# Head norms by a ScalarE square root, attention's loads on GpSimd's queue and plain stick-breaking gates in a decoder block

## The chip, the cores and the metric

One core of a Trainium2 chip runs the whole program. The metric is the device time of one execution in microseconds; the time of a kernel is the median of its runs. TensorE is PE (its weight loads PEld), VectorE is DVE, ScalarE is ACT, GpSimd is POOL, and SyncE, which only issues DMAs here, is SP.

## The reference

One decoder block with D = 1024 on 1024 positions in float32. Three branches work on the normed input in parallel, are gated and summed, and an MLP follows.

```python
proj = einsum('bsd,de->bse', rmsnorm(x, g_mix_norm), w_in)
sb_q, sb_k, sb_v, fx_q, fx_k, fx_v, f_logit, m_q, gate_logit = split_columns(proj, SPLITS)
o_sb = stick_breaking_attention(heads(sb_q), heads(sb_k), heads(sb_v))        # 8 heads of 64
fq, fk = rmsnorm(heads(fx_q), g_fox_q), rmsnorm(heads(fx_k), g_fox_k)
o_fox = forgetting_attention(fq, fk, heads(fx_v), log_sigmoid(f_logit + b_forget))  # 8 of 64
mk, mv = split(einsum('bmd,de->bme', rmsnorm(mem, g_mem_norm), w_mem_kv))     # 256 tokens
o_mem = memory_attention(rmsnorm(heads(m_q), g_mem_q), rmsnorm(mk, g_mem_k), mv)  # 4 of 128
gates = sigmoid(gate_logit)                                                   # 3 x 1024
merged = gates[0] * (o_sb @ w_branch_sb) + gates[1] * (o_fox @ w_branch_fox) + gates[2] * (o_mem @ w_branch_mem)
x = x + merged @ w_out
u = relu(rmsnorm(x, g_mlp_norm) @ w_ff_up);  x = x + (u * u) @ w_ff_down
```

The root of the change is the one in `rmsnorm` of the heads of fx_q, fx_k, m_q and mk.

## The kernel before

**Products.** Each float32 operand is split in a high and a low part (`split`, L1046 and L1047: a copy on ACT, a subtraction on DVE), and a product is three passes on PE: high by high, high by low, low by high. A weight block of 128 x 1024 is fetched raw (`fetch`, L1054), then split into `whi` and `wlo`.

**Stages** in the profiled execution: the norm of x and its transposes with the first values (0 to 50 us), the keys and values of the memory (to 120), six projections `sbk, sbq, mq, fxk, fxq, sbv` (to 385) by seven products each instead of eight (`KINDS`, matmuls at L1412; their weight blocks come by `unit_loads`, L1335), attention (to 905), two branch products (to 1000), the third branch (`last_branch`, to 1100), the output product, the MLP up (L1840, to 1450) and down (L2510, to the end). Head pairs 0 to 3 are stick-breaking, 4 to 7 forgetting; the products of the gates (`dense_gate`, L1133) and the memory's attention run between them and fill PE.

**Order.** All stages up to the branches are written as coroutines in a planner. A coroutine asks for an engine with an estimated cost (`Op`), for a buffer out of a pool (`Get`), for an event, or for time to pass (`Sleep`); the planner simulates these and so writes the order of the instructions of each engine. That order is fixed at build time. On the chip an engine takes its instructions in this order, and an instruction whose semaphores are late holds all behind it. `spawn(gen, late)` gives a coroutine a priority, a lower number being earlier. `transfer` (L298) issues a DMA on SP and tells the planner when it should have landed. An `Op` for a table function of ACT adds 1.3 us to the plan when the table has to change.

**The heads' norm** (`normed_turned`, L711) takes a 128 x 512 tile of sums of squares `st` (reduced at L707) and `rsqrt_ops` makes the inverse root: an integer seed on DVE (L351, L352), then three Newton steps of four operations on POOL (L358 to L361). DVE scales the tile (L716), PE turns it by four transposes (L723), ACT and DVE split it (L729, L730). The norm of x uses `root` and `rsqrt_quick` instead: a square root on ACT (L369) and a reciprocal with one correcting step on DVE (L374 to L383).

**Loads of attention.** The turned keys and queries go through DRAM (`sbk_scr` and others). `load_pairs` (L996) fetches them for each pair and half in pieces of 64 x 512, 128 KB, into places of the pool HT; `load_v` (L1032) fetches the pair's values once all of them are stored (L1207). The output of a unit is evicted to a buffer `ob` (L956, pool OB with 2 buffers) and stored by SP (L959). Gates are evicted to `o` (L1533, `gate_put`), as a sigmoid for gates 0 to 7 and 16 to 23, plain for 8 to 15, and stored to `gate_scr` (L1537); the branches load them back. All of these issue on SP.

Of the kernel before, what the change touches and what calls it, by code (L numbers as in the profile page):

```python
# [16 lines left out]
I32 = mybir.dt.int32  # L17
# [26 lines left out]
def tile_hybrid_block(  # L44
# [253 lines left out]
    def transfer(fn, size, issue=0.1, rate=250e3):  # L298

        yield Op("SP", issue, fn, 0.0)  # L300
        machine.pipe = max(machine.now, machine.pipe) + size / rate
        yield Sleep(machine.pipe + 2.0 - machine.now)
# [42 lines left out]

    def rsqrt_ops(ss, n):

        v, y0, a_, y1 = stat(n), stat(n, I32), stat(n), stat(n)

        def seed():  # L350
            nc.vector.tensor_scalar(v, ss, EPS, None, ALU.add)  # L351
            nc.vector.tensor_scalar(y0, v.bitcast(I32), -0.5, 1597463007.0, ALU.mult, ALU.add)  # L352
        yield Op("DVE", 2 * SMALL, seed)

        def steps():
            a, b = y0.bitcast(F32), y1
            for _ in range(3):
                nc.gpsimd.tensor_tensor(a_, a, a, ALU.mult)  # L358
                nc.gpsimd.tensor_tensor(a_, a_, v, ALU.mult)  # L359
                nc.gpsimd.tensor_scalar(a_, a_, -0.5, 1.5, ALU.mult, ALU.add)  # L360
                nc.gpsimd.tensor_tensor(b, a_, a, ALU.mult)  # L361
                a, b = b, a
        yield Op("POOL", 12 * 0.2, steps)
        return y1
# [214 lines left out]
    def memory():  # L579
        yield pairs[4].made[1]  # L580

        def fetched_q(h, half):
            q = yield Get(HT, 2)

            def issue():
                for t, scr in zip(q, p_scr["mq"]):
                    nc.sync.dma_start(f32(t), scr[h * P:(h + 1) * P, half * 512:(half + 1) * 512])
            yield from transfer(issue, 2 * P * 512 * 4, 0.2)
            q_of[h, half] = q
        q_of = {}  # L590
        for c in range(2):
# [3 lines left out]
            def issue():  # L595
                for i, t in enumerate(kv):
                    nc.sync.dma_start(f32(t), m_scr[c][:, i, :])
            loaded = spawn(transfer(issue, 4 * P * 512 * 4, 0.4), -20.0)
# [112 lines left out]
    def normed_turned(raw, ss, hd, gain, fn):  # L711

        n = 512 // hd
        r = yield from rsqrt_ops(ss, n)
        raw3 = raw.rearrange("p (n d) -> p n d", d=hd)
        yield Op("DVE", dve_time(512), lambda: nc.vector.tensor_tensor(  # L716
            raw3, raw3, r.unsqueeze(2).to_broadcast([P, n, hd]), ALU.mult))
        tr = yield Get(TR)
# [122 lines left out]
    def fox_tile(pair, b, i, e):  # L841
# [8 lines left out]
        def chunk(ci, c, cols, u):  # L850
# [14 lines left out]
            yield Op("ACT", act_time(u) + 0.17, lambda: nc.scalar.activation(  # L865
# [110 lines left out]
    def load_pairs():  # L976
        yield ready
        for c, pair in enumerate(pairs):
# [5 lines left out]
            for b in range(2):  # L984
# [4 lines left out]
                def halves(half):  # L989
# [5 lines left out]
                    def put(k, rows_, src):  # L995
                        nc.sync.dma_start(f32(t[k][rows_, :]), src)  # L996
# [19 lines left out]
                evs = [spawn(transfer(k0_, 4 * HD * 2048, 0.3), -20.0), spawn(transfer(k1_, 4 * HD * 2048, 0.3), -20.0),  # L1016
# [1554 lines left out]
```

## Time and profile before

| | before |
|---|---|
| median of 3 runs | 1763.73 us (1763.01 to 1766.23) |
| profiled execution | 1765.67 us |
| its span, mean granted clock | 1763.9 us, 0.992 |
| PE busy | 1708.9 us |
| ACT busy | 895.2 us |
| POOL busy | 172.9 us |
| ACT table loads L1533, x10 | 12.8 us |

The span is the time from the first to the last instruction of one profiled execution. Busy times of engines overlap, so they do not add to the span. A wait in a view is the idle time of an engine just before an instruction, with the instruction or DMA whose semaphore came last. The granted clock is that of PE in a stretch, 1.00 being full speed.

### The profile page before, as it was taken

How to read it: one execution, taken by the hardware profiler on the slowest of the kernel's cores; microseconds unless marked ns; L12 is line 12 of the kernel's file. 1: busy time of each engine (PE TensorE's matmuls, PEld its weight loads, DVE VectorE, ACT ScalarE, POOL GpSimd, SP SyncE). 2: the span in 40 equal slices, each digit the busy share in tenths (PEclk: the TensorE clock that was granted, in tenths of full speed). 3: DMA queues.
4: the chain of work that ended last, by engine and by line, in shares of the span. 5: the costliest groups of instructions: out<-in, count | busy, mean ns of one | idle time of the engine just before them, and what ended most of it. 6: DMA issues, size and time to landing. Idle time of an engine off the chain costs nothing.

```text
span 1763.9 us, 25496 instructions
## 1 busy us (share of the span) xinstructions
PE 1708.9 (97%) x9186; PEld 1450.5 (82%) x9186; DVE 1338.7 (76%) x2243; ACT 895.2 (51%) x1612; POOL 172.9 (10%) x445
## 2 busy tenths in 40 slices
PE   9989988897999999999999999999999999999999
PEld 8978988896888888788888887878888887888887
DVE  7875677756998976688875789897777777687875
ACT  6443354444676699888862235733333344333331
POOL 0010165500000000000000001112111220000000
PEclk9999999998999999999999999999999999999999
DMA  6544432556545433653556743134444467365531
GB/s 234 176 141 156 145 105 90 164 177 199 141 120 146 142 98 109 180 164 99 160 153 208 239 169 115 53 120 159 158 144 148 144 235 261 132 209 182 199 119 72
DMA packets 175694, 271.72 MB, mean 154 GB/s; under 512 B 14992, under 2 KB 88720, under 8 KB 175568
## 3 DMA queue, kind: packets, MB, share of 16 engines
q1 hardware_dynamic: 165712, 237.33, 42.1%
q0 software_dynamic: 9856, 32.78, 5.3%
q8 instruction: 72, 1.18, 0.3%
q14 instruction: 54, 0.44, 0.1%
HBM read 181.44 MB, written 88.60 MB: 153 GB/s over the span
## 4 chain that ended last, share of the span: by engine, by line
PE 53%; issue 15%; POOL 8%; DVE 6%; DMA 3%; ACT 3%; SPq 1%; POOLq 0%; ACTq 0%; DVEq 0%
PE pp L1133 17%; PE pp L2510 7%; PE tr L2510 3%; PE sc L2510 3%; POOL s_scr L1857 3%; PE tr L921 3%; PE pv L2510 2%; PE pv L938 2%; PE sc L938 2%; POOL st L358 1%; PE pp L1840 1%; POOL st L359 1%; POOL st L360 1%; POOL st L361 1%; DVE h L1776 1%
## 5 line engine op out<-in xcount | busy, mean ns | idle before, releaser
L1133 PE MATMUL pp<-hi,whi 128*128 128x512 f32 x368 | 148.8, 404 | 0.0
L1133 PE MATMUL pp<-lo,whi 128*128 128x512 f32 x368 | 145.9, 396 | 0.0
L1133 PE MATMUL pp<-hi,wlo 128*128 128x512 f32 x368 | 145.5, 395 | 0.0
L1047 DVE TENSOR_TENSOR wlo<-raw,whi 128x1024 fp32r<-128x1024 f32 (+1 forms) x82 | 100.1, 1221 | 45.6 <-ACT whi L1046 45.5
L1046 ACT ACTIVATE whi<-raw 128x1024 fp32r<-128x1024 f32 (+1 forms) x82 | 86.4, 1056 | 87.8 <-DMA raw<-w_b 35.1
L2510 PE MATMUL pp<-h,sop 128*128 128x512 f32 x540 | 128.7, 395 | 1.1 <-DVE sop L1776 1.1
L2510 PEld LDWEIGHTS pp<-h,sop 128*128 128x128 f32 x540 | 101.1, 187 | 26.2 <-DVE sop L1776 1.6
L1840 PE MATMUL pp<-h,oh 128*128 128x512 f32 x384 | 120.9, 396 | 0.7 <-ACT cu L1926 0.6
L928 DVE TENSOR_TENSOR ptl<-tr,pth 128x512 fp32r<-128x512 f32 (+1 forms) x160 | 98.6, 627 | 21.3 <-ACT pth L926 20.1
L926 ACT ACTIVATE pth<-tr 128x512 fp32r<-128x512 f32 (+1 forms) x160 | 86.3, 559 | 19.8 <-PE tr L921 7.9
L831 DVE TENSOR_TENSOR_SCAN r<-r,sm 128x896 f32<-128x896 f32 (+5 forms) x64 | 85.6, 1346 | 7.9 <-ACT r L816 7.9
L1840 PEld LDWEIGHTS pp<-h,oh 128*128 128x128 f32 x384 | 71.8, 187 | 19.2 <-ACT cu L1926 1.5
L2428 ACT ACTIVATE h<-t 128x2048 fp32r<-128x2048 f32 x16 | 30.7, 1919 | 110.2 <-DVE t L1776 97.4
L2111 POOL TENSOR_TENSOR h<-h,gb 128x512 f32<-128x512 f32 x8 | 12.0, 1502 | 750.9 <-DMA x_scr<-h 750.9
L1133 PEld LDWEIGHTS pp<-hi,wlo 128*128 128x128 f32 x368 | 69.6, 189 | 16.7
L1133 PEld LDWEIGHTS pp<-hi,whi 128*128 128x128 f32 x368 | 70.1, 190 | 10.0
L1133 PEld LDWEIGHTS pp<-lo,whi 128*128 128x128 f32 x368 | 70.1, 190 | 10.0
L1840 PE MATMUL pp<-h,ol 128*128 128x512 f32 x192 | 76.0, 396 | 0.0
L1833 ACT ACTIVATE oh<-raw 128x512 fp32r<-128x512 f32 x64 | 39.4, 625 | 61.8 <-DVE raw L1776 61.8
L2510 PE MATMUL sc<-h,sop 128*128 128x512 f32 x264 | 63.4, 395 | 0.0
L2510 PE MATMUL tr<-h,sop 128*128 128x512 f32 x264 | 63.4, 395 | 0.0
L1133 PE MATMUL pp<-h,whi 128*128 128x512 f32 x192 | 63.0, 396 | 0.0
(615 smaller groups left out, 5071.7 us busy)
## 6 DMA issues: line engine op xcount, KB each, us to landing
ur<-s_scr SPq DMA_DIRECT2D x26, 1024.0 KB
raw<-w_in SPq DMA_DIRECT2D x50, 512.0 KB
raw<-w_up SPq DMA_DIRECT2D x60, 256.0 KB
s_scr<-s POOLq DMA_DIRECT2D x60, 256.0 KB, 2.5
g<-w_down SPq DMA_DIRECT2D x14, 1024.0 KB
s_scr<-cu POOLq DMA_DIRECT2D x48, 256.0 KB, 2.9
gate_scr<-o SPq DMA_DIRECT2D x46, 256.0 KB
o<-gate_scr SPq DMA_DIRECT2D x32, 256.0 KB
```

The costliest lines, as they stand in the source:

```text
L831: nc.vector.tensor_tensor_scan(out=rev, data0=rev, data1=zero.to_broadcast([P, n]), initial=1.0, op0=ALU.mult, op1=ALU.add)
L921: nc.tensor.transpose(tr[:, jj * 256 + a * P:jj * 256 + (a + 1) * P], es[a][:, j * P:(j + 1) * P], ident)
L926: yield Op("ACT", act_time(512 - lo_c), lambda: nc.scalar.activation(ph[:, lo_c:], tr[:, lo_c:], AF.Copy))
L928: yield Op("DVE", dve_time(512 - lo_c), lambda: nc.vector.tensor_tensor(pl[:, lo_c:], tr[:, lo_c:], f32(ph[:, lo_c:]), ALU.subtract))
L938: nc.tensor.matmul(pv[0][:, c_:256], pair.v[:, j, b, :], p_[:, jj * 256 + c_:(jj + 1) * 256], start=(k == 0 and n_ == 0 and i == 0), stop= ...
L1046: yield Op("ACT", 0.03 + act_time(m), lambda: nc.scalar.activation(hi, raw, AF.Copy))
L1047: yield Op("DVE", dve_time(m), lambda: nc.vector.tensor_tensor(lo, raw, f32(hi), ALU.subtract))
L1133: nc.tensor.matmul(ps, a_, b_, start=(first and i == 0), stop=(last and i == n - 1))
L1833: nc.scalar.activation(h_, src, AF.Copy)
L1840: nc.tensor.matmul(ps, w[a_][:, k * P:(k + 1) * P], h[b_][k], start=(first and k == 0 and i == 0), stop=(last and k == 3 and i == 2), skip ...
L1857: nc.gpsimd.dma_start(s_scr[r0:r0 + P, :], t)
L2510: nc.tensor.matmul(ps, a_[:, c, qs], b_[:, c, :], start=(kind in ("P1", "P2", "P7") and c == 0 and i == 0), stop=(kind in ("P2", "P4", "P3 ...
```

## The change

1. `rsqrt_ops` goes; `normed_turned` calls `root` on ACT and `rsqrt_quick` on DVE. The planner waits 0.8 us before it asks for the buffer of the transposes.
2. The DMAs of attention's keys, queries and values, the memory's, the projections' weight blocks, and the raw weight blocks once the memory's keys and values are made are issued by POOL. The planner's costs of an issue change with it.
3. Gates 0 to 7 are stored plain as well; the branch of stick-breaking (b == 0) takes the sigmoid after it has loaded the gate.
4. `ob` has three buffers in place of two; the memory's attention waits for the end of pair 3 in place of the keys of pair 4; `forget` starts two projections earlier; `unit_prep` has priority -4; the second load of the root table becomes a square root that reads `raw1[0]`; the planner's estimate of an exponential goes from 0.17 to 0.21.

```diff
-    def transfer(fn, size, issue=0.1, rate=250e3):
-        yield Op("SP", issue, fn, 0.0)
+    def transfer(fn, size, issue=0.1, rate=250e3, queue_="SP"):
+        yield Op(queue_, issue, fn, 0.0)
         machine.pipe = max(machine.now, machine.pipe) + size / rate
...
         return ((a[0], b[0]), (a[0], b[1]), (a[1], b[0]))
-    def rsqrt_ops(ss, n):
-        v, y0, a_, y1 = stat(n), stat(n, I32), stat(n), stat(n)
-        def seed():
-            nc.vector.tensor_scalar(v, ss, EPS, None, ALU.add)
-            nc.vector.tensor_scalar(y0, v.bitcast(I32), -0.5, 1597463007.0, ALU.mult, ALU.add)
-        yield Op("DVE", 2 * SMALL, seed)
-        def steps():
-            a, b = y0.bitcast(F32), y1
-            for _ in range(3):
-                nc.gpsimd.tensor_tensor(a_, a, a, ALU.mult)
-                nc.gpsimd.tensor_tensor(a_, a_, v, ALU.mult)
-                nc.gpsimd.tensor_scalar(a_, a_, -0.5, 1.5, ALU.mult, ALU.add)
-                nc.gpsimd.tensor_tensor(b, a_, a, ALU.mult)
-                a, b = b, a
-        yield Op("POOL", 12 * 0.2, steps)
-        return y1
...
     def memory():
-        yield pairs[4].made[1]
+        yield pairs[3].over
...
                 for t, scr in zip(q, p_scr["mq"]):
-                    nc.sync.dma_start(f32(t), scr[h * P:(h + 1) * P, half * 512:(half + 1) * 512])
-            yield from transfer(issue, 2 * P * 512 * 4, 0.2)
+                    nc.gpsimd.dma_start(f32(t), scr[h * P:(h + 1) * P, half * 512:(half + 1) * 512])
+            yield from transfer(issue, 2 * P * 512 * 4, 1.1, queue_="POOL")
             q_of[h, half] = q
...
                 for i, t in enumerate(kv):
-                    nc.sync.dma_start(f32(t), m_scr[c][:, i, :])
-            loaded = spawn(transfer(issue, 4 * P * 512 * 4, 0.4), -20.0)
+                    nc.gpsimd.dma_start(f32(t), m_scr[c][:, i, :])
+            loaded = spawn(transfer(issue, 4 * P * 512 * 4, 2.2, queue_="POOL"), -20.0)
             evs = []
...
         n = 512 // hd
-        r = yield from rsqrt_ops(ss, n)
+        z = stat(n)
+        yield Op("ACT", 0.25, lambda: root(z, ss), table=AF.Sqrt)
+        r = yield from rsqrt_quick(ss, z, n)
         raw3 = raw.rearrange("p (n d) -> p n d", d=hd)
...
             raw3, raw3, r.unsqueeze(2).to_broadcast([P, n, hd]), ALU.mult))
+        yield Sleep(0.8)
         tr = yield Get(TR)
...
             yield Op("DVE", (0.22 if c + u == n else 0.0) + dve_time(u) + SMALL, maxima)
-            yield Op("ACT", act_time(u) + 0.17, lambda: nc.scalar.activation(
+            yield Op("ACT", act_time(u) + 0.21, lambda: nc.scalar.activation(
                 e[:, c:c + u], sc[:, :u], AF.Exp, bias=nx[:, ci:ci + 1], accum_out=l[:, ci:ci + 1]), table=AF.Exp)
...
                     def put(k, rows_, src):
-                        nc.sync.dma_start(f32(t[k][rows_, :]), src)
+                        nc.gpsimd.dma_start(f32(t[k][rows_, :]), src)
                     lower, upper, f4 = slice(0, HD), slice(HD, P), slice(HD, HD + 4)
...
                 (k1_, q1_), (k0_, q0_) = halves(1), halves(0)
-                evs = [spawn(transfer(k0_, 4 * HD * 2048, 0.3), -20.0), spawn(transfer(k1_, 4 * HD * 2048, 0.3), -20.0),
-                       spawn(transfer(q1_, (3 if fox else 2) * HD * 2048, 0.3), -20.0),
-                       spawn(transfer(q0_, (3 if fox else 2) * HD * 2048, 0.3), -20.0)]
+                evs = [spawn(transfer(k0_, 4 * HD * 2048, 1.6, queue_="POOL"), -20.0), spawn(transfer(k1_, 4 * HD * 2048, 1.6, queue_="POOL"), -20.0),
+                       spawn(transfer(q1_, (3 if fox else 2) * HD * 2048, 1.2, queue_="POOL"), -20.0),
+                       spawn(transfer(q0_, (3 if fox else 2) * HD * 2048, 1.2, queue_="POOL"), -20.0)]
                 if b == 0:
...
         h0 = 2 * (pair.p % 2)
-        yield from transfer(lambda: nc.sync.dma_start(f32(pair.v), src[:, :, h0:h0 + 2, :]), P * 8192)
+        yield from transfer(lambda: nc.gpsimd.dma_start(f32(pair.v), src[:, :, h0:h0 + 2, :]), P * 8192, 0.8, queue_="POOL")
         machine.fire(pair.v_made)
...
-    def fetch(raw, load):
+    def fetch(raw, load, queue_=nc.sync):
         pieces, kk, n = load
...
             m = src.shape[1]
-            nc.sync.dma_start(view[:, :, off:off + m], src.rearrange("(k p) n -> p k n", p=P))
+            queue_.dma_start(view[:, :, off:off + m], src.rearrange("(k p) n -> p k n", p=P))
...
             raw = yield Get(RAW)
-            yield from transfer(lambda: fetch(raw, load), P * kk * n * 4)
+            if kv_over.fired:
+                yield spawn(transfer(lambda: fetch(raw, load, nc.gpsimd), P * kk * n * 4, 0.8, queue_="POOL"), -30.0)
+            else:
+                yield from transfer(lambda: fetch(raw, load), P * kk * n * 4)
         else:
...
-        yield prepped["fxk", "P1"]
+        yield prepped["sbq", "P1"]
         for ev in logits_made:
...
                 def fetched_block(u=u, key=key, raw=raw, src=src):
-                    yield from transfer(lambda: nc.sync.dma_start(
-                        raw.rearrange("p (k n) -> p k n", k=4), src.rearrange("(k p) n -> p k n", p=P)), P * 4096)
+                    yield from transfer(lambda: nc.gpsimd.dma_start(
+                        raw.rearrange("p (k n) -> p k n", k=4), src.rearrange("(k p) n -> p k n", p=P)), P * 4096, 0.8,
+                        queue_="POOL")
                     machine.fire(block_in[u, key])
...
         E.close()
-        opened("A2", (PH, "pth", 2, 512, F32R), (PL, "ptl", 2, 512, F32R), (OB, "ob", 2, 256, F32),
+        opened("A2", (PH, "pth", 2, 512, F32R), (PL, "ptl", 2, 512, F32R), (OB, "ob", 3, 256, F32),
                (ES, "es", 4, 512, F32), (OO, "o", 3, 512, F32), (HT, "h", 7, 512, F32R))
+        yield Sleep(4.0)
         pair = yield Get(WP)
...
             gt = yield Get(place)
-            func = AF.Copy if KD <= n < 2 * KD else AF.Sigmoid
+            func = AF.Copy if n < 2 * KD else AF.Sigmoid
             yield Op("ACT", act_time(512), lambda: nc.scalar.activation(gt, ps, func),
...
                     gts[d, half], gate_scr[b * D + d * P:b * D + (d + 1) * P, half * 512:half * 512 + 512]), P * 512 * 4)
+                if b == 0:
+                    yield Op("ACT", act_time(512), lambda: nc.scalar.activation(gts[d, half], gts[d, half], AF.Sigmoid),
+                             table=AF.Sigmoid)
...
         spawn(unit_loads())
-        spawn(unit_prep())
+        spawn(unit_prep(), -4.0)
         spawn(forget(), 5.0)
...
     early = []
-    root_table()
+    nc.scalar.activation(C.t("st", [P, 8])[:, :1], raw1[0][:, :1], AF.Sqrt, bias=one, scale=0.0)
...
```

How the order of instructions moves, at three places.

DVE, in the projections, at one head norm of the forgetting keys. `sn` is the tile, `st` its sums and roots, `wlo` the low part of a weight block. Before:

```order
L707 TENSOR_REDUCE st_1163<-sn_146 128x4
L351 TENSOR_SCALAR st_1181<-st_1163 128x4
L352 TENSOR_SCALAR st_1182<-st_1181 128x4
L1047 TENSOR_TENSOR wlo_164<-raw_166,whi_163 128x1024
L716 TENSOR_TENSOR sn_145<-sn_145,st_1184 128x512
```

After the change:

```order
L687 TENSOR_REDUCE st_1163<-sn_146 128x4
L354 TENSOR_SCALAR st_1202<-st_1163 128x4
L357 RECIPROCAL st_1181<-st_1181 128x4
L361 TENSOR_TENSOR st_1203<-st_1181 128x4
L362 TENSOR_TENSOR st_1203<-st_1203,st_1202 128x4
L363 SCALAR_TENSOR_TENSOR st_1204<-st_1203,st_1181 128x4
L1030 TENSOR_TENSOR wlo_164<-raw_166,whi_163 128x1024
L698 TENSOR_TENSOR sn_145<-sn_145,st_1204 128x512
```

The two operations before POOL's twelve have become five that end the root on DVE itself, and the split of a weight block still stands ahead of the scaling.

SP, at the start of attention. `h` are the places of the pair's keys and queries, `v_sb` the stored values in DRAM, `raw` a weight block. Before:

```order
L996 DMA h_4094<-sbq_scr_86 64x512
L996 DMA h_4091<-sbq_scr_85 64x512
L996 DMA h_4091<-sbq_scr_86 64x512
L1207 DMA v_sb_96<-sn_138 128x512
L1207 DMA v_sb_96<-sn_145 128x512
L1207 DMA v_sb_95<-sn_140 128x512
L1207 DMA v_sb_95<-sn_139 128x512
L1207 DMA v_sb_95<-sn_143 128x512
L1207 DMA v_sb_95<-sn_144 128x512
L1032 DMA v_4103<-v_sb_95 128x8x256
```

After the change the loads stand on the queue of POOL:

```order
L1037 DMA raw_166<-w_in 128x8x128
L979 DMA h_3873<-sbk_scr_87 64x512 x2
L979 DMA h_3872<-sbk_scr_88 64x512 x2
L979 DMA h_3876<-sbk_scr_87 64x512 x2
L979 DMA h_3875<-sbk_scr_88 64x512 x2
L979 DMA h_3874<-sbq_scr_85 64x512
L979 DMA h_3874<-sbq_scr_86 64x512
L979 DMA h_3871<-sbq_scr_85 64x512
L979 DMA h_3871<-sbq_scr_86 64x512
L1015 DMA v_3883<-v_sb_95 128x8x256
L1037 DMA raw_165<-w_in 128x8x128
```

The twelve loads of the pair have left SP, where the value stores stood behind them; the weight block `raw_165` is still behind the value load, now on POOL.

POOL, at the start of the program. Before, the masks are followed by the first head norm:

```order
L105 AFFINE_SELECT above<-above 128x129
L358 TENSOR_TENSOR st_1183<-st_1182 128x4
L359 TENSOR_TENSOR st_1183<-st_1183,st_1181 128x4
L360 TENSOR_SCALAR st_1183<-st_1183 128x4
L361 TENSOR_TENSOR st_1184<-st_1183,st_1182 128x4
```

After the change the projections' weight blocks follow them:

```order
L105 AFFINE_SELECT above<-above 128x129
L1321 DMA raw_147<-w_in 128x4x256
L1321 DMA raw_148<-w_in 128x4x256
L1321 DMA raw_149<-w_in 128x4x256
L1321 DMA raw_150<-w_in 128x4x256
```

On SP these four stood behind the loads of x and the stores of the first values; on POOL nothing stands ahead of them but the masks.

## The prediction

> **What bounds the kernel now.** I read the page's first two parts, then the PE waits of the whole run, then the windows by stage, then the lines and the timeline of the stages in which PE waits.
>
> ```profile
> PE 1708.9 (97%) x9186; PEld 1450.5 (82%) x9186; DVE 1338.7 (76%) x2243; ACT 895.2 (51%) x1612; POOL 172.9 (10%) x445
> PEclk9999999998999999999999999999999999999999
> ```
>
> TensorE is the bound: 1708.9 of 1763.9 us busy, and the change leaves its products as they are. So a gain can come only from the 55 us in which PE is idle and from the stretches at a lower granted clock (the 8 in the tenth slice). The waits say who ends the idle time (line, total, times, longest):
>
> ```profile
> PE tr L723 <- DVE sn L716: 12.9, 18, 1.9
> PE pp L812 <- ACT e L817: 12.2, 2, 7.5
> PE tr L723 <- DVE sn L730: 3.7, 2, 2.1
> PE sc L1133 <- ACT pth L675: 3.4, 1, 3.4
> PE pp L854 <- ACT r L641: 1.6, 1, 1.6
> PE tr L723 <- DVE st L351: 1.3, 1, 1.3
> PE sc L854 <- DMA h<-fxk_scr: 1.0, 1, 1.0
> ```
>
> Two groups carry it: the head norms of the projections (L723) and the starts of attention (L812, L1133, L854). The stages, as start:end, length, then busy us of PE, PEld, DVE, ACT, POOL, then clock, DMA share and GB/s:
>
> ```profile
> 0.00:20.00 20.00, 16.55 (x127) 15.72 (x128) 12.09 (x32) 12.47 (x22) 1.09 (x8) 1.00 0.95 331
> 180.00:385.00 205.00, 187.05 (x1494) 180.32 (x1493) 140.54 (x225) 93.90 (x139) 89.51 (x289) 0.99 0.42 129
> 385.00:450.00 65.00, 52.84 (x273) 44.50 (x272) 43.04 (x63) 33.55 (x72) 0.00 (x0) 0.89 0.62 186
> 600.00:900.00 300.00, 293.58 (x1707) 251.97 (x1706) 233.87 (x696) 262.78 (x615) 0.00 (x0) 0.99 0.45 134
> ```
>
> In the projections PE is idle for 18 of 205 us, in the first 65 us of attention for 12, at a clock of 0.89. From 600 to 900 PE leaves only 6.4 us.
>
> **Part 1, the roots.** The root of before stands between the reduction and DVE's scaling L716: two small DVE operations, twelve POOL operations, then L716.
>
> ```profile
> L716 DVE TENSOR_TENSOR sn<-sn,st 128x512 f32<-128x512 f32 x24 | 16.6, 692 | 29.0 <-POOL st L361 28.9
> L358 POOL TENSOR_TENSOR st<-st 128x8 f32<-128x8 f32 (+1 forms) x78 | 26.4, 338 | 239.9 <-DVE st L352 234.1 <-DVE st L351 1.7
> L359 POOL TENSOR_TENSOR st<-st,st 128x8 f32<-128x8 f32 (+1 forms) x78 | 23.8, 305 | 6.1
> L361 POOL TENSOR_TENSOR st<-st,st 128x8 f32<-128x8 f32 (+1 forms) x78 | 23.5, 302 | 6.5
> L360 POOL TENSOR_SCALAR st<-st 128x8 f32<-128x8 f32 (+1 forms) x78 | 22.4, 288 | 6.8
> ```
>
> 78 of each line are 26 roots of three steps: 96.1/26 = 3.7 us of POOL each, and DVE itself stands idle for 28.9 us behind it. The new root is one ACT square root and five small DVE operations, as the x norm already has them:
>
> ```profile
> L369 ACT ACTIVATE st<-st,sm x11: 283/296/298, 5.8 to 1129.4; 128x2 f32<-128x2 f32 x7, 128x1 f32<-128x1 f32 x4
> L374 DVE TENSOR_SCALAR st<-st x11: 145/160/170, 5.8 to 1130.4; 128x2 f32<-128x2 f32 x7, 128x1 f32<-128x1 f32 x4
> L377 DVE RECIPROCAL st<-st x11: 153/163/166, 6.2 to 1131.1; 128x2 f32<-128x2 f32 x7, 128x1 f32<-128x1 f32 x4
> L381 DVE TENSOR_TENSOR st<-st x7: 160/161/161, 24.3 to 1131.3; 128x2 f32<-128x2 f32 x7
> ```
>
> That is 0.30 + 5 × 0.16 = 1.1 us in place of some 4. DVE gets three small operations more per root (26 × 3 × 0.16 = 12 us over stages in which it has 205 − 140.54 = 64 us free), ACT 26 × 0.30 = 8 us of 111 free; both are hidden. The waits that the POOL chain ends, 12.9 + 1.3 = **14.2 us**, I take as gone. The 3.7 us behind L730 is a place in the transposes' buffer and stays. Bounds: where the new chain stands on ACT and DVE behind a weight block's split (1.06 and 1.22 us below), half a microsecond at each of 18 waits may stay, so −5; at the other end L730's wait goes too, and the 0.01 of clock over 205 us, so −14.2 − 3.7 − 2 = −20.
>
> **Part 2, loads on POOL's queue.** L812's two waits, 12.2 us, are for ACT's exponentials, and ACT stands in order behind a weight block's split or an eviction whose DMA is late:
>
> ```profile
> 401.21 1.06 ACT L1046 ACTIVATE whi<-raw 128x1024 fp32r<-128x1024 f32 x1 [6.92 <-DMA raw<-w_in]
> 425.25 1.06 ACT L1046 ACTIVATE whi<-raw 128x1024 fp32r<-128x1024 f32 x1 [4.34 <-DMA raw<-w_in]
> 431.56 0.38 ACT L956 ACTIVATE ob<-sc 64x256 f32<-64x256 f32 x1 [4.24 <-DMA o_scr<-ob]
> 719.81 0.38 ACT L956 ACTIVATE ob<-pv 64x256 f32<-64x256 f32 x1 [4.99 <-DMA o_scr<-ob]
> ```
>
> SP's queue at the first of these places (start, length, engine, transfer, count) shows why:
>
> ```profile
> 374.96 5.17 SPq L996 DMA_DIRECT2D h<-sbk_scr  x8
> 380.17 2.51 SPq L996 DMA_DIRECT2D h<-sbq_scr  x4
> 382.78 3.91 SPq L1207 DMA_DIRECT2D v_sb<-sn  x6
> 389.52 0.59 SPq L1032 DMA_DIRECT2D v<-v_sb  x1
> 391.33 0.94 SPq L1054 DMA_DIRECT2D raw<-w_in  x1
> 428.99 0.54 SPq L959 DMA_DIRECT2D o_scr<-ob  x1
> ```
>
> A 128 KB load takes about 0.63 us to issue (7.68/12). The value stores wait behind twelve of them, the whole value load waits for those stores, and the weight block follows it; the output's store at 428.99 comes behind a pair's loads in the same way. With the loads on POOL the stores run alone on SP, so the value load can start some 7.7 us sooner, and an output's store no longer stands behind loads. A third `ob` buffer allows one more store in flight. All four waits of PE here add up to 12.2 + 3.4 + 1.6 + 1.0 = 18.2 us, and the lower clock to at most 0.11 × 65 = 7.2 us, together 25.4. The added waits are on POOL: each load there waits for a free destination, and the next pair's loads, the memory's and the weight blocks stand behind it; weight blocks are placed ahead, but the second still stands behind a value load. So I take not all: **−20**, the idle time and a quarter of the clock's share; bounds 0 (the waits move onto POOL's queue) and −25.4.
>
> How long POOL needs to issue one is in the rows of the later stages:
>
> ```profile
> L1857 POOL DMA_DIRECT2D s_scr<-s x60: 540/540/542, 1178.6 to 1449.1; - x60
> L1857 POOL DMA_DIRECT2D s_scr<-cu x48: 540/540/727, 1150.4 to 1448.4; - x48
> ```
>
> 540 ns, at most 727, with DVE busy beside it: no dearer than SP. 176 attention loads, 8 values, 24 of the memory, 29 weight blocks and 24 projection blocks are 261 × 0.54 = 141 us of an engine that has no other work then. The Trainium skill ("SBUF — State Buffer", section "A bandwidth-pool intuition that's wrong") speaks against it: GpSimd must write the descriptors of its own queue, and DVE's two-port operations lock it out, so that an issue grows from some 620 ns to 3100. By that page 237 issues would be an estimated 0.73 ms of POOL over the 520 us of attention and the loads would bound it; the 108 issues above do not show that, but they are small and few, so the rule is the last rival below.
>
> **Part 3, startup.** The first four projection blocks wait for nothing in the changed order and stand first on POOL. Before, they were issued at 48.6 us:
>
> ```profile
> 48.62 3.22 SPq L1335 DMA_DIRECT2D raw<-w_in  x4
> ```
>
> Now 2.1 MB compete with x and the first weights, in 20 us in which the DMA is full (0.95, 331 GB/s). 2.1 MB / 331 GB/s = 6.3 us if all of it goes ahead of what PE needs, 0 if none. The rows give no order between the queues; as both have something to move throughout, I take two thirds, **+4**.
>
> **Part 4, gates and tables.** Gates 0 to 7 are now copied like 8 to 15, and the sigmoid comes back as 16 ACT operations in the branch stage at 950–1000.
>
> ```profile
> L1533 ACT ACTIVATE o<-pp 128x512 f32<-128x512 f32 x46 | 27.6, 600 | 14.0 <-PE pp L1133 10.1 <-DMA v_sb<-sn 3.5
> L1533 ACT ACT_TABLE_LOAD x10 | 12.8, 1283 | 0.2
> 900.00:1000.00 100.00, 100.00 (x456) 81.79 (x455) 60.45 (x88) 29.16 (x45) 0.00 (x0) 1.00 0.62 194
> ```
>
> The order has 33 table loads before and 14 after: 19 × 1.28 = 24 us of ACT, nearly all in attention. It is worth little there, as PE leaves only 6.4 us of that stage and ACT 37; I count **0**, at best the 5 us of PE's waits not already counted. The 16 sigmoids, 16 × 0.60 = 9.6 us, fall where ACT is idle for 71 of 100 us; a gate's product waits for its load plus 0.6 us. I take **+1** for them and for two further table loads (sqrt, then sigmoid again) in the last branch; bounds 0 and 16 × 0.60 + 2 × 1.28 = +12. Dropping POOL's cover costs nothing: nothing else ran on it then.
>
> **Sum.** −14.2 − 20 + 4 + 1 = −29.2 us on the profiled execution of 1765.67 us (span 1763.9), 1736.5. The median of the runs, 1763.73, lies 1.9 below it, so the forecast of a median is **1735**. With all bounds at one end it is 1763.73 − 50 = 1713, at the other 1763.73 − 5 + 6.3 + 12 = 1777.
>
> **Rivals.** A measurement of this kernel tells about 0.2%, 3.5 us, from no change.
> - B: the head-of-line wait moves to POOL's queue, since a pair's loads wait for buffers there and the weight block behind them. For: the second block still follows the value load. Against: SP's stores are out of the way. Only the roots and the small terms remain: 1763.73 − 14.2 + 5 = 1754.5.
> - C: all idle time of both groups goes, the startup's blocks find gaps, and the freed ACT takes another 5 us: 1763.73 − 14.2 − 25.4 − 5 = 1719. For: every transfer that these waits end on moves to a queue of its own; against: a DMA share of 0.95 in the first 20 us, and no row that shows POOL's queue with such loads.
> - D, slower: POOL is held up by DVE at each issue. POOL's arithmetic shows such a hold beside a weight block's split:
>
> ```profile
> 246.29 1.22 DVE L1047 TENSOR_TENSOR wlo<-raw,whi 128x1024 fp32r<-128x1024 f32 x1
> 246.48 1.08 POOL L358 TENSOR_TENSOR st<-st 128x4 f32<-128x4 f32 x1
> ```
>
>   1.08 us is 0.74 more than that line's mean of 0.338. An issue would take 0.54 + 0.74 = 1.28, and the twelve loads ahead of a pair would end 12 × 0.74 = 8.9 us later. With three such heads exposed (first pair, first forgetting pair, memory), no gain of part 2, and the small terms: 1763.73 − 14.2 + 5 + 27 = 1781.5. It decides once more than one head is exposed (8.9 against 9.2 of gain). Against: the 540 ns rows. For: they stand beside another mix of DVE work. The skill's rule named above is this rival, and in its full size later still.
> - E: no change, as the roots' waits reappear behind ACT's order, and the loads': 1763.
>
> **Chances.** Forecast 0.50, B 0.15, C 0.14, D 0.17, E 0.04. The forecast's own range is 1722 to 1750; 8 in 10 needs B and C, and part of E: 1713 to 1763. Faster by over 0.2%: 0.50 + 0.15 + 0.14 = 0.79; within: 0.04; slower: 0.17.
>
> **What would show it.** Part 1: PE's waits on L723 fall from 18 us to under 5, and DVE no longer idles before L716's successor. Part 2: no idle of 4 us or more on ACT before the split or the `ob` eviction between 385 and 450, and a clock near 1 there; POOL's issue rows at 540 ns confirm, over 1 us refute. Part 3: PE's first 20 us end later by 0 to 6 us. Part 4: 14 table loads, no DVE wait on the new sigmoid that ends in a PE wait. The forecast is wrong if PE waits for weight blocks or `h` loads inside attention, or if a stall at the head of attention is as long as before under another name.

## The result and the profile after

The changed kernel takes **1719.84 us** (median of 4 runs, 1717.76 to 1721.22); the kernel before, run beside it, 1764.98 us. The ratio is 0.9741, with a 95% interval of 0.9721 to 0.9761. The profiled execution took 1721.22 us, its span is 1719.1 us. That is inside the range and 15 us below the number forecast.

The busy times, the clock and the PE waits of the whole run, after the change:

```profile
PE 1696.8 (99%) x9186; PEld 1446.4 (84%) x9186; DVE 1345.3 (78%) x2321; ACT 886.0 (52%) x1635; POOL 261.1 (15%) x446
PEclk9999999999999999999999999999999999999999
```

```profile
PE pp L1119 <- ACT hi L459: 5.4, 1, 5.4
PE pp L1399 <- DVE wlo L1030: 3.1, 1, 3.1
PE pp L1119 <- DVE g L1642: 2.0, 1, 2.0
PE pp L1119 <- DVE wlo L1030: 1.7, 4, 0.8
PE pv L401 <- POOL ident masks.py:199: 1.5, 1, 1.5
```

PE's idle time has fallen from 55 us to 22, and neither of the two groups of before is in the list: no wait on the transposes of the head norms, none on an exponential, a probability or an `h` load. What is new is one wait of 5.4 us on ACT, at startup, and one of 2.0 us at 875 us, in the branch products, where DVE's product with the gate (`g`) stands behind the split of a late weight block. The windows of before over the last four of the six projections (`mq` to `sbv`, which hold the three with a head norm; from their first product to their last) and attention:

```profile
191.40:385.40 194.00, 176.05 (x1449) 171.54 (x1448) 132.57 (x215) 89.05 (x132) 89.51 (x289) 0.99 0.41 126
385.40:912.10 526.70, 508.12 (x2934) 437.28 (x2933) 422.35 (x986) 408.70 (x930) 0.00 (x0) 0.98 0.48 142
```

PE was idle for 18.0 us of the first and 18.6 of the second. The startup of the changed kernel, the same four projections, the first 65 us of attention behind them, and a later stretch of attention:

```profile
0.00:20.00 20.00, 11.41 (x69) 10.12 (x70) 6.36 (x17) 8.68 (x15) 4.25 (x12) 0.87 0.93 320
196.60:365.60 169.00, 169.00 (x1441) 169.00 (x1440) 132.02 (x275) 86.24 (x146) 16.83 (x26) 1.00 0.49 154
365.60:430.60 65.00, 65.00 (x370) 56.01 (x369) 56.47 (x85) 46.20 (x98) 29.64 (x54) 1.00 0.69 209
580.00:850.00 270.00, 270.00 (x1618) 234.92 (x1617) 220.33 (x684) 228.18 (x578) 75.21 (x134) 1.00 0.44 136
```

PE is busy for every microsecond of the four projections and of both stretches of attention, at full clock. Cut at the same products, the spans compare like this (in what follows, "the projections" are these last four):

| stretch | before | after | difference | forecast |
|---|---|---|---|---|
| start to the first product of `mq` | 191.4 | 196.6 | +5.2 | +4 |
| the last four projections | 194.0 | 169.0 | −25.0 | −14.2 |
| attention to the end | 1378.5 | 1353.5 | −25.0 | −19 |
| span | 1763.9 | 1719.1 | −44.8 | −29.2 |

Three terms came as forecast in sign, and two were too small. The runs below ask what the projections' second eleven microseconds are, and whether attention's gain is the queue's.

### The profile page after: what moved, and what is told of

It reads as the page before. It is cut to its first block, busy times and chain, and to the rows that moved or that the text cites. A ratio compares the mean times of both kernels' runs of the same rounds, so it can differ in the third digit from the quotient of the medians.

```text
span 1719.1 us, 25350 instructions
## 1 busy us (share of the span) xinstructions
PE 1696.8 (99%) x9186; PEld 1446.4 (84%) x9186; DVE 1345.3 (78%) x2321; ACT 886.0 (52%) x1635; POOL 261.1 (15%) x446
## 5 line engine op out<-in xcount | busy, mean ns | idle before, releaser
L909 ACT ACTIVATE pth<-tr 128x512 fp32r<-128x512 f32 (+1 forms) x160 | 86.7, 558 | 29.2 <-PE tr L904 15.1
L814 DVE TENSOR_TENSOR_SCAN r<-r,sm 128x896 f32<-128x896 f32 (+4 forms) x64 | 85.5, 1344 | 3.8 <-ACT r L799 3.7
L1767 DVE TENSOR_TENSOR sop<-ur,sop 128x2048 fp32r<-128x2048 f32 x27 | 61.7, 2284 | 1.7 <-ACT sop L2430 1.7
```

What stands on the lines that cost most here:

```text
L814: nc.vector.tensor_tensor_scan(out=rev, data0=rev, data1=zero.to_broadcast([P, n]), initial=1.0, op0=ALU.mult, op1=ALU.add)
L909: yield Op("ACT", act_time(512 - lo_c), lambda: nc.scalar.activation(ph[:, lo_c:], tr[:, lo_c:], AF.Copy))
L1767: nc.vector.tensor_tensor(out_, a_, b_, op)
```

## Experiments

Each kernel was timed in three rounds beside the kernel before. The column of the projections is the length of the last four, the next what follows them, both from one profiled execution each.

| kernel | median us | ratio, 95% interval | projections | rest |
|---|---|---|---|---|
| roots | 1746.57 | 0.9897, 0.9882 to 0.9912 | 181.3 | 1373.7 |
| roots_late | 1753.03 | 0.9916, 0.9891 to 0.9942 | 186.1 | 1372.9 |
| roots_forget | 1734.71 | 0.9822, 0.9804 to 0.9839 | 169.1 | 1374.6 |
| roots_edits | 1734.05 | 0.9818, 0.9800 to 0.9836 | 169.0 | 1371.6 |
| queue | 1741.88 | 0.9873, 0.9857 to 0.9889 | 194.2 | 1354.1 |
| queue_only | 1741.64 | 0.9869, 0.9845 to 0.9893 | 194.4 | 1360.8 |
| costs_only | 1752.54 | 0.9920, 0.9905 to 0.9934 | 194.2 | 1365.7 |
| roots_queue | 1728.20 | 0.9778, 0.9757 to 0.9799 | 181.5 | 1355.6 |
| sp_true | 1722.54 | 0.9749, 0.9727 to 0.9772 | 169.0 | 1355.6 |
| gates | 1765.82 | 1.0008, 0.9997 to 1.0018 | 193.7 | 1378.3 |
| old_gates | 1719.40 | 0.9729, 0.9704 to 0.9753 | 169.0 | 1351.3 |
| blocks_sp | 1713.38 | 0.9706, 0.9691 to 0.9720 | 169.0 | 1351.2 |

### The projections: the root alone

```diff
-        r = yield from rsqrt_ops(ss, n)
+        z = stat(n)
+        yield Op("ACT", 0.25, lambda: root(z, ss), table=AF.Sqrt)
+        r = yield from rsqrt_quick(ss, z, n)
```

> The kernel before with the new root alone (ScalarE square root and five VectorE operations in place of the POOL chain; nothing else moved by hand). In the changed kernel the matmuls of the projections lost 24.1 us of time above their undisturbed pace (25.5 to 1.4), where the prediction took 14.2. Theory: the root alone brings all 24, the waits behind L730 and the half clock included: 1765 - 24 = 1741 us, PE's waits on the transposes under 3 us, attention's stalls as before. Rival: the root brings the 14.2 us of its own waits, and the rest comes from the planner's small edits (the 0.8 us before the transposes, the priority -4): 1751 us with 3 to 8 us of waits left on the transposes.

Measured 1746.57 us, about midway between the theory's 1741 and the rival's 1751. In the projections it took 12.7 us (194.0 to 181.3). What follows them became shorter as well, by 4.8 us (1378.5 to 1373.7), though the edit touches nothing there. PE's waits in the projections, from 190 to 372 us of this kernel:

```profile
PE pp L1414 <- ACT sn L1450: 3.3, 2, 2.1
PE pp L1414 <- DVE wlo L1049: 3.2, 2, 2.7
PE tr L725 <- DVE sn L732: 0.2, 1, 0.2
```

The transposes no longer wait: 0.2 us where there were 17.9. But PE now waits elsewhere, for an eviction on ACT and a block's split. ACT around the first of these, in the timeline (start, length, instruction, idle time before it):

```profile
299.84 0.60 ACT L1450 ACTIVATE sn<-pp 128x512 f32<-128x512 f32 x1 [3.95 <-DMA fxk_scr<-sn]
310.84 1.06 ACT L1048 ACTIVATE whi<-raw 128x1024 fp32r<-128x1024 f32 x1 [3.93 <-PE pp L1414]
314.18 0.69 ACT L731 ACTIVATE sn<-tr,sm 128x512 fp32r<-128x512 f32 x1 [1.79 <-DMA fxk_scr<-sn]
```

ACT waits for tile buffers `sn` whose stores by SP have not landed. At that time the forgetting sums (`forget`: the cumulated logarithms of the forgetting gates, stored to `fq_scr` and `fk_scr`) take `sn` tiles, too, and issue their small stores on SP. Such a wait can cost more than its idle time: behind the one that ends at 306 us PE runs for 3.5 us at a granted clock of 0.52.

```profile
306.50:310.00 3.50, 3.50 (x19) 3.50 (x18) 1.82 (x6) 0.41 (x1) 0.51 (x1) 0.52 0.37 121
```

### The planner's edits with the root

Two edits are added to the root: the pause ahead of the transposes, and the blocks' preparation at priority −4.

```diff
+        yield Sleep(0.8)
-        spawn(unit_prep())
+        spawn(unit_prep(), -4.0)
```

> The kernel before with the new root, the 0.8 us of planner's time ahead of the transposes and priority -4 for the blocks' preparation; loads and gates as before. The root alone gave 1746.6 us and left four stalls of PE in the projections, 7.1 us at 245, 304, 311 and 338 us (behind ACT's eviction L1450 and DVE's split L1049). Theory: these are matters of order that the two planner edits settle, 1746.6 - 7 to 9 = 1738 to 1740 us. Rival: the eviction waited 4.0 us for a store of the keys on SP, so they need the loads off SP, 1745 to 1747 us.

Measured 1753.03 us: both expectations failed. The two edits do not help the root by themselves; the median is higher than the root's (the intervals overlap), and the projections are 4.8 us longer. PE's idle time there is nearly all in two waits on the transposes, which end at 305.2 and 312.3 us:

```profile
PE tr L726 <- DVE sn L733: 11.0, 2, 5.9
306.90 0.69 ACT L732 ACTIVATE sn<-tr,sm 128x512 fp32r<-128x512 f32 x1 [4.54 <-DMA fk_scr<-sn]
311.48 0.75 DVE L733 SCALAR_TENSOR_TENSOR sn<-tr,sm,sn 128x512 fp32r<-128x512 f32 x1 [6.30 <-DMA fk_scr<-sn]
```

Here the tile that ACT and DVE wait for is one of the forgetting sums' own (`fk_scr`). SP at that place:

```profile
303.04 0.35 SPq L1301 DMA_DIRECT2D fk_scr<-sn  x1
304.35 0.26 SPq L1302 DMA_DIRECT2D fk_scr<-sn  x1
309.31 0.29 SPq L1315 DMA_DIRECT2D fk_scr<-sn  x1
309.65 0.29 SPq L1316 DMA_DIRECT2D fk_scr<-sn  x1
310.04 6.15 SPq L1504 DMA_DIRECT2D fxk_scr<-sn  x5
```

The first two of these stores stand ahead of ACT's wait, the next two ahead of DVE's, and the keys' stores come behind them all. The next kernel takes the root and the third edit, the earlier start of the sums, and nothing else:

```diff
     def forget():
 
-        yield prepped["fxk", "P1"]
+        yield prepped["sbq", "P1"]
```

> The new root and the earlier start of the forgetting sums alone (they wait for the second projection's first block in place of the fourth's). The root alone gave 1746.6 us; two of its stalls, 3.6 us, and half a clock behind them lie at 304 and 311 us, where these sums take ACT, tile buffers and a dozen small stores on SP. Theory: they go, and with the half clock 4 to 7 us: 1740 to 1743 us. Rival: the stalls are of the projections' own evictions and stay: 1745 to 1748.

Measured 1734.71 us, better than the theory's 1740. The projections take 169.1 us, as in the changed kernel. The sums' copies, in the root alone and here (x4: min/median/max ns, first and last start):

```profile
L1302 ACT ACTIVATE sn<-sn x4: 612/616/631, 252.2 to 301.9; 8x512 fp32r<-8x512 f32 x4
```

```profile
L1302 ACT ACTIVATE sn<-sn x4: 612/614/635, 159.5 to 187.6; 8x512 fp32r<-8x512 f32 x4
```

The window over the projections of this kernel:

```profile
191.80:360.90 169.10, 169.09 (x1440) 168.88 (x1439) 131.92 (x275) 85.08 (x145) 0.52 (x1) 1.00 0.47 145
```

They have left the stage, and PE is busy for 169.09 of its 169.10 us. So, added in this order, the gain of 24.9 us in the projections is 12.7 for the root and 12.2 for the sums' earlier place. The stores are not all that the sums bring. Their exponential and logarithm need other tables of ACT than the new root, and in the root alone seven table loads, 9.0 us of ACT, fall in this stage (L1284 is the sums', L369 the root), in this kernel one:

```profile
L1284 ACT ACT_TABLE_LOAD x4 | 5.1, 1283 | 0.1
L369 ACT ACT_TABLE_LOAD x3 | 3.8, 1283 | 0.0
```

The waits shown end on stores; how much of the 12.2 us the table loads add by making ACT later was not tried apart. With all three edits:

```diff
-        yield prepped["fxk", "P1"]
+        yield prepped["sbq", "P1"]
...
+        yield Sleep(0.8)
-        spawn(unit_prep())
+        spawn(unit_prep(), -4.0)
```

> The new root with the earlier start of the forgetting sums, the 0.8 us ahead of the transposes and priority -4 together. Without the earlier sums the two other edits made the root slower (1753.0 in place of 1746.6, stalls of 5.2 and 6.3 us at 300 and 306). Theory: that was the sums' place too, and together they bring the projections to what the changed kernel has, no stall over 0.5 us between 200 and 360: 1738 to 1742 us. Rival: the two edits cost by themselves, and it is slower than with the sums alone: 1744 or more.

Measured 1734.05 us: on the theory's side and below its range, and the same as without the two small edits. What they seemed to cost in `roots_late` was the sums' place, too. Whether the earlier sums help while the root is still on POOL was not tried.

### Attention: the queue and the planner's costs

Loads of attention, memory and raw weight blocks on POOL, with the planner's dearer costs, and nothing else:

```diff
-                        nc.sync.dma_start(f32(t[k][rows_, :]), src)
+                        nc.gpsimd.dma_start(f32(t[k][rows_, :]), src)
...
-                evs = [spawn(transfer(k0_, 4 * HD * 2048, 0.3), -20.0), spawn(transfer(k1_, 4 * HD * 2048, 0.3), -20.0),
+                evs = [spawn(transfer(k0_, 4 * HD * 2048, 1.6, queue_="POOL"), -20.0), spawn(transfer(k1_, 4 * HD * 2048, 1.6, queue_="POOL"), -20.0),
```

> The kernel before with attention's and the memory's loads and the raw weight blocks on POOL's queue alone; POOL roots, sigmoid gates, two ob buffers and the projections' blocks on SP stay. Theory: attention's stalls are a matter of SP's queue, and all 26 us of them go: 1739 us, ACT never idle over 2 us on a weight block between 385 and 450. Rival 1: the stalls at about 665 and 840 us, with ACT full of table loads, stay: 1765 - 26 + 6 = 1745. Rival 2: with POOL's queue the weight block still stands behind the value load and only a part goes: 1750 or more.

Measured 1741.88 us, between the theory and its first rival. What follows the projections falls from 1378.5 to 1354.1, 24.4 us, nearly all of the changed kernel's 25.0. The start of attention in this kernel:

```profile
385.50:450.50 65.00, 64.08 (x361) 54.68 (x361) 55.22 (x84) 44.76 (x96) 29.54 (x54) 1.00 0.69 208
```

64.08 of 65 us busy, where it was 52.84, and the clock is 1.00 instead of 0.89. ACT's idle time ahead of a weight block's split fell from 11.3 to 1.6 us in this window, as the theory asked. All that follows the projections, in the kernel before and in this one:

```profile
385.40:1763.90 1378.50, 1351.39 (x6579) 1116.03 (x6577) 1066.78 (x1802) 716.22 (x1333) 75.53 (x124) 0.99 0.48 155
385.50:1739.60 1354.10, 1344.77 (x6578) 1112.85 (x6577) 1066.23 (x1802) 716.73 (x1333) 234.14 (x400) 1.00 0.48 157
```

Of the 24.4 us, 17.8 are idle time of PE (27.1 to 9.3), and 6.6 are busy time: the same products ran faster. Between this kernel and the changed one 0.6 us are left for the root, the third `ob` buffer, the memory's place and the plain gates together, less than the runs of one kernel differ. The root and the queue together:

```diff
+        yield Op("ACT", 0.25, lambda: root(z, ss), table=AF.Sqrt)
+        r = yield from rsqrt_quick(ss, z, n)
...
+                        nc.gpsimd.dma_start(f32(t[k][rows_, :]), src)
```

> The new root and attention's loads on POOL's queue together, without the planner edits, the gates, the third ob buffer and the projections' blocks on POOL. Alone they gave -18.5 and -23.2 us. Theory: they add, 1765 - 41.7 = 1723 us, with the four stalls of the projections still there. Rival: the projections' remaining stalls come from the raw weight blocks on SP and go with the queue: 1714 to 1717 us. Other rival: they overlap, since the root alone had already shortened attention's stalls (9.3 in place of 12.2 us): 1726 or more.

Measured 1728.20 us, in the range of the overlap (1726 or more) and 5 us above the sum; the intervals of the ratios alone would still allow the sum. The stages show the overlap: the projections keep the root's length, 181.5, and the rest the queue's, 1355.6, so the 4.8 us that the root alone took there do not come on top of the queue's 24.4.

To tell SP's queue from the planner's costs, the changed kernel has these loads back on SP, at the dearer costs:

```diff
-                        nc.gpsimd.dma_start(f32(t[k][rows_, :]), src)
+                        nc.sync.dma_start(f32(t[k][rows_, :]), src)
...
-                evs = [spawn(transfer(k0_, 4 * HD * 2048, 1.6, queue_="POOL"), -20.0), spawn(transfer(k1_, 4 * HD * 2048, 1.6, queue_="POOL"), -20.0),
+                evs = [spawn(transfer(k0_, 4 * HD * 2048, 1.6, queue_="SP"), -20.0), spawn(transfer(k1_, 4 * HD * 2048, 1.6, queue_="SP"), -20.0),
```

> The changed kernel with attention's, the memory's and the weight blocks' loads issued by SP again, but with the planner told the dearer issue costs; the projections' blocks stay on POOL. Theory: the queue is the cause, as a pair's loads again hold the stores and the value load: 1735 to 1746 us and ACT idle for 3 us or more on a weight block or an ob store near the start of attention. Rival: the planner's better costs are the cause, the queue only a name: 1718 to 1722 us.

Measured 1722.54 us: **the theory of the queue fell** in the form in which it was stated. Its sign on ACT came, a wait of 3.5 us for a weight block near the start of attention, but not its time. SP's queue at the head of attention reads nearly as before the change:

```profile
355.79 4.98 SPq L979 DMA_DIRECT2D h<-sbk_scr  x8
360.81 2.51 SPq L979 DMA_DIRECT2D h<-sbq_scr  x4
363.42 5.22 SPq L1193 DMA_DIRECT2D v_sb<-sn  x8
369.85 0.59 SPq L1015 DMA_DIRECT2D v<-v_sb  x1
370.48 0.66 SPq L1037 DMA_DIRECT2D raw<-w_in  x1
```

Twelve loads, then the stores, the value load and the block, all in one row, and yet PE waits there for only 4.3 us in the first 65 us of attention, not 12.2:

```profile
PE sc L795 <- ACT es L800: 2.5, 1, 2.5
PE pp L795 <- ACT e L800: 1.8, 2, 1.4
```

Two runs on the kernel before ask for each of the two alone. In both, as in `queue` and in the changed kernel, the raw weight blocks also leave from a process of their own at priority −30; that edit was not tried by itself. The costs alone, on SP:

```diff
-                evs = [spawn(transfer(k0_, 4 * HD * 2048, 0.3), -20.0), spawn(transfer(k1_, 4 * HD * 2048, 0.3), -20.0),
+                evs = [spawn(transfer(k0_, 4 * HD * 2048, 1.6, queue_="SP"), -20.0), spawn(transfer(k1_, 4 * HD * 2048, 1.6, queue_="SP"), -20.0),
```

> The kernel before with the planner's dearer issue costs alone (1.6, 1.2, 0.8, 1.1 and 2.2 us where it had 0.3, 0.1, 0.2 and 0.4, weight blocks in a process of their own); every load still on SP. On the changed kernel, taking the loads back to SP with these costs cost only 2.7 us, so the theory that SP's queue is the cause is in doubt. New theory: the costs are the cause, because the order that they write puts PE's products where the loads really land: 1740 to 1746 us. Old theory, the queue: 1755 to 1766. Third: either of the two suffices: 1740 to 1746 here, and the same with the queue alone.

Measured 1752.54 us, neither the one theory nor the other: 13.5 us of gain, about half. The start of attention:

```profile
385.50:450.50 65.00, 61.71 (x332) 51.75 (x331) 51.04 (x77) 39.31 (x85) 0.00 (x0) 0.97 0.78 220
```

At this place, with every load on SP, 3.3 of the 12.2 us of waits are left and the clock is 0.97; most of what the costs do not bring lies later. The order on SP did change a little: the weight block is now issued ahead of the value load (388.15 and 389.27 us), where it came behind it. And the queue alone, with the old costs:

```diff
-                        nc.sync.dma_start(f32(t[k][rows_, :]), src)
+                        nc.gpsimd.dma_start(f32(t[k][rows_, :]), src)
...
-                evs = [spawn(transfer(k0_, 4 * HD * 2048, 0.3), -20.0), spawn(transfer(k1_, 4 * HD * 2048, 0.3), -20.0),
+                evs = [spawn(transfer(k0_, 4 * HD * 2048, 0.3, queue_="POOL"), -20.0), spawn(transfer(k1_, 4 * HD * 2048, 0.3, queue_="POOL"), -20.0),
```

> The kernel before with the same loads on POOL's queue, but with the planner's old cheap issue costs. New theory, the costs are the cause: 1755 to 1766 us, with a stall of PE of 3 us or more near the start of attention. Old theory, the queue: 1740 to 1745 us. Third: either suffices: 1740 to 1745 too, and then the run with the costs alone has to be as fast.

Measured 1741.64 us: the old theory's time, and as much as queue and costs together. Its profiled execution, at 1749.17 us, was the longest of its four runs and has one wait of 3.9 us left on L812's products, the stall that the new theory named, so the 1360.8 in the table overstates its rest. So the queue suffices without the costs, and the costs without the queue bring half. With the other edits beside them the costs on SP bring nearly all (1355.6 against 1353.5). Which of those edits makes up the other half was not tried apart; the root with the planner's edits, on the old costs and SP, already shortens the rest by 6.9 us (1371.6, `roots_edits`).

### The gates, and the blocks at startup

```diff
-            func = AF.Copy if KD <= n < 2 * KD else AF.Sigmoid
+            func = AF.Copy if n < 2 * KD else AF.Sigmoid
...
+                if b == 0:
+                    yield Op("ACT", act_time(512), lambda: nc.scalar.activation(gts[d, half], gts[d, half], AF.Sigmoid),
+                             table=AF.Sigmoid)
```

> The kernel before with the gates 0 to 7 stored plain and the sigmoid in the branch alone. Theory: ACT's table loads fall from 33 to about 15, some 23 us of ACT, and the time stays: 1762 to 1766 us, as PE is not waiting for ACT in the full stretches. Rival: the late stalls (3.4 us at L1133 and 1.6 at L854, and their half clock) are ACT's lateness from table loads, and go: 1757 to 1759.

Measured 1765.82 us, ratio 1.0008: no change. ACT's table loads fell from 33 to 13. The rival's stall of 3.4 us at L1133 is gone, and of the 1.6 at L854 0.8 are left, but waits of 6.4 us on L921's transposes have come: the order moved and the time did not. The same edit undone in the changed kernel:

```diff
-            func = AF.Copy if n < 2 * KD else AF.Sigmoid
+            func = AF.Copy if KD <= n < 2 * KD else AF.Sigmoid
...
-                if b == 0:
-                    yield Op("ACT", act_time(512), lambda: nc.scalar.activation(gts[d, half], gts[d, half], AF.Sigmoid),
-                             table=AF.Sigmoid)
```

> The changed kernel with gates 0 to 7 as a sigmoid again and no sigmoid in the branch. Theory: ACT pays some 20 table loads more, about 25 us, but PE does not wait for them: 1718 to 1723 us. Rival: with the other stalls gone, ACT at 44 of 50 us from 600 to 800 becomes the bound and the table loads show: 1726 to 1735 us.

Measured 1719.40 us against 1719.84: no change either, with 34 table loads in place of 14. The 20 table loads, some 25 us of ACT's time, are worth nothing that these runs can measure, with the stalls of before and without them.

The changed kernel with the projections' blocks back on SP:

```diff
-                    yield from transfer(lambda: nc.gpsimd.dma_start(
-                        raw.rearrange("p (k n) -> p k n", k=4), src.rearrange("(k p) n -> p k n", p=P)), P * 4096, 0.8,
-                        queue_="POOL")
+                    yield from transfer(lambda: nc.sync.dma_start(
+                        raw.rearrange("p (k n) -> p k n", k=4), src.rearrange("(k p) n -> p k n", p=P)), P * 4096)
```

> The changed kernel with the projections' weight blocks back on SP, where the first four are issued after the loads of x. Theory: the 4.3 us by which the changed kernel reaches 120 us late are these four blocks' share of a full DMA, and come back: 1720 - 4.3 = 1715.5 us, PE busy 9.8 us instead of 4.3 from 10 to 20 us. Rival: on SP the blocks of the later projections come behind stores and PE waits for them there: 1718 to 1722.

Measured **1713.38 us** (ratio 0.9706, below the changed kernel's 0.9741 with intervals that just part), the fastest of all. The first split of a weight block on ACT in the changed kernel, and in this one:

```profile
15.48 1.06 ACT L1029 ACTIVATE whi<-raw 128x1024 fp32r<-128x1024 f32 x1 [5.52 <-DMA raw<-w_in]
```

```profile
9.38 1.06 ACT L1029 ACTIVATE whi<-raw 128x1024 fp32r<-128x1024 f32 x1
...
48.47 2.59 SPq L1321 DMA_DIRECT2D raw<-w_in  x4
```

The second row there is the four projection blocks, now issued at 48.47 us. The first 20 us of this kernel as a window:

```profile
0.00:20.00 20.00, 16.58 (x126) 15.75 (x127) 12.02 (x32) 12.38 (x22) 1.10 (x8) 1.00 0.95 331
```

With the four blocks, 2.1 MB, issued 47 us earlier than on SP, the first weight block was split 6.1 us later. With them back on SP, PE is busy for 16.58 of the first 20 us, not 11.41. The projections are reached 4.6 us sooner (192.0 in place of 196.6 us). The rival's later waits on SP did not come: the projections are as long as with POOL, 169.0.

## Why the prediction was right and wrong

- **Sign, range and bound.** PE's idle time and lost clock were the only place for a gain, and that is where it came from; the range of 1713 to 1763 held the time, the forecast's own range of 1722 to 1750 missed it by 2 us. The number of rival C, 1719, came, but by luck, not by its sum: it had the startup hidden, which cost 5, the projections at 14, which gave 25, and 5 for the freed ACT, which no run shows.
- **Part 1, the root: right by itself, in part by luck.** It was put at 14.2 and measured 12.7 in its stage. That L730's 3.7 us would stay was wrong, since 0.2 is left; it was balanced by new waits of 6.5 us, which go when the sums start earlier. That it also takes 4.8 us behind the projections was not foreseen.
- **The step that failed** is that the earlier start of `forget` was not costed at all. The bound of 20 us for the stage was drawn from PE's waits on the old root and its clock, as if no other edit touched the projections. The runs put 12.2 us there, which makes the stage's gain 10.8 us larger than forecast; the span's whole miss is 15.6 (44.8 against 29.2). The clock's term in that bound, 0.01 of 205 us, was too small as well: PE's busy time in the stage fell by 7.05 us, from 176.05 to 169.00, of which the sums' own eight transposes, which left the stage, are at most 8 × 0.27 = 2.2. What to look for were ACT's waits on late stores of `sn` tiles. In the kernel before ACT has such waits in this stage:

```profile
ACT sn L1448 <- DMA fxk_scr<-sn: 2.2, 1, 2.2
ACT sn L729 <- DMA fxk_scr<-sn: 1.9, 1, 1.9
```

  That more of them lay beneath PE's wait on the root there is an inference, as no run took the sums away with the old root.
- **Part 2, loads: right in sign, mis-sized.** 20 were taken out of 25.4, and 25.0 came; the table's 19 is with Part 4's microsecond. The idle time was right, 18.2 against 17.8 by the queue. The term that was too small is the clock's: a quarter of its 7.2 us was taken, 1.8, and PE's busy time fell by 6.6. The mechanism was half right. Taking the loads and the weight blocks off SP is enough without the costs. But nearly the same order on SP hurts little at the head of attention once the planner is told dearer costs, so "late because it stands behind" was not the whole of it. That the planner then puts PE's products where the loads land is the likely reason, and is not shown.
- **Part 3, startup: right.** +4 forecast, +5.2 in the profile; the blocks' return gave 0.35% of the time, some 6 us, between the two medians, of which 4.6 lie in this stretch.
- **Part 4, gates and tables: right.** 0 and +1 forecast; both runs cannot be told from no change, and +1 is too small for them.
- **Rival D fell.** POOL's issues of the pair's loads, with DVE beside them at 56 of 65 us:

```profile
L979 POOL DMA_DIRECT2D h<-sbk_scr x52: 522/524/552, 332.7 to 491.2; - x52
L979 POOL DMA_DIRECT2D h<-fxk_scr x46: 522/528/567, 500.4 to 776.7; - x46
L979 POOL DMA_DIRECT2D h<-fxq_scr x39: 522/538/572, 520.4 to 780.8; - x39
```

  None takes over 0.572 us. The Trainium skill ("SBUF — State Buffer", section "A bandwidth-pool intuition that's wrong") has a DMA of this queue grow from some 620 to 3100 ns beside a VectorE `tensor_copy`. No row of this queue shows that beside this mix of DVE work; whether any of it holds the port as that copy does, no run shows, so the rows speak against rival D here and not against the page.

## What to carry to other kernels

Where an order is fixed ahead of time, a wait that PE shows on one operation can cover another that is equally late: cost every edit that touches the stage, the "small" changes of a start condition above all, and read who holds buffers and queues there. Truer issue costs in the plan and an emptier queue can be two remedies for one stall, so do not add their gains. Count what PE's busy time loses to a lower clock behind a wait, and not the idle time alone. A load that waits for nothing should still not be issued while the DMA is full of what is needed first (a share of 0.93 here).

## What the runs showed of the hardware

One operation of POOL's own arithmetic took 1.08 us beside a weight block's split on DVE, in the prediction's rows, against a median of 0.198 for its line; the mean of 0.338 there holds other such long ones. Its DMA issues were not stretched: 522 to 572 ns for a load of 128 KB in the rows of L979 above, where SP took a median of 593 ns for the `sbk_scr` loads in `sp_true`. A 512 KB block took 0.75 us to issue on POOL as 128x4x256 and 0.92 us as 128x8x128.

```profile
L1321 POOL DMA_DIRECT2D raw<-w_in x24: 748/748/917, 1.7 to 308.7; - x24
L1037 POOL DMA_DIRECT2D raw<-w_in x23: 882/923/1035, 309.5 to 817.6; - x23
```
